# TensorE's instructions of the expert groups in one written order

## The chip, the cores and the metric

The kernel runs on one core of one Trainium2 chip. The time is the device time of one execution in microseconds (us). The core's engines, as the profile names them: TensorE (PE; the loads of its stationary operands are shown apart, as PEld), VectorE (DVE), ScalarE (ACT), GpSimd (POOL) and SyncE (SP), which issues the transfers of the weights from HBM to the on-chip memory over the DMA engines. Each engine has its own queue of instructions and works through it in order; where one engine needs a result of another, it waits at a semaphore.

## The reference, cut to what matters

Two layers (DEPTH = 2) work on x of 256 tokens x 1024 channels, all in fp32. In each, a mixer of three branches (a state-space scan, a gated spatial MLP, attention to 256 memory tokens) is added to x, then a mixture of experts, each followed by a LayerNorm. The change lies in the mixture of experts:

```python
D_MODEL, SEQ, N_GROUPS_MOE, EXP_PER_GROUP, D_EXPERT, TOP_K_INNER = 1024, 256, 4, 8, 256, 2

g_star = argmax(x @ w_rg + b_rg)                 # one of 4 groups for each token
top_v, top_i = top_k(le_sel, 2)                  # two of its 8 experts
weights = softmax over the group's choice and the two experts, zero for all others
h = silu(einsum('nd,edf->nef', x, w_gate_e)) * einsum('nd,edf->nef', x, w_up_e)
moe = einsum('nef,efd->nd', h * weights[:, :, None], w_down_e)
x = layer_norm(alpha * x + moe)
```

There are 32 experts. Each has 1024 x 256 weights for the gate, as many for the up product and 256 x 1024 for the down product: 3 MB, so 100 MB a layer, and every one is read in both layers.

## The kernel before, in words

A layer (the variable l) first computes the mixers, which fill the first half of its time, and then the experts. The **expert stage** takes the experts in 8 groups of four (the loop over g, NG = 8). Each expert has 32 slots for tokens, so that a group's 128 slots fill the 128 partitions.

**Weights.** A group's weights are 12 pieces of 128 x 2048 numbers, 1 MB each: 8 pieces for gate and up (w_gu, k = 0 to 7) and 4 for down (w_dn, two for each half hf of the 1024 output channels). `Stream` (L98 to 170) keeps the list of all pieces in order, and SP issues the DMA of a piece as soon as the ring of buffers that it belongs to has one free; `RINGS` (L188) deals the pieces out to 23 such places, in rotation. `st.done` gives a buffer free, and the next piece's DMA is issued at that place of the program.

**One group.** In the order in which the code is written:

- `pick` (L1208): VectorE writes a matrix of zeros and ones, M.S, that says which token stands in which slot (L1214, L1216).
- `gather` (L1227): TensorE multiplies it by x, 16 matmuls in the program for two halves of the channels (32 in the trace, since each fp32 matmul runs as two passes); ScalarE (L1237) and VectorE (L1239) each copy one half out of its bank of PSUM (in groups 0 and 1 they share each half, column block by column block).
- `columns` (L1258): the products with one piece, 4 matmuls of 32 x 512 in the program and 8 in the trace, one for each expert. Eight pieces add up in one bank (`hb`). After the fourth, `place_back` (L1218) turns M.S around and scatters the weights of the tokens to their slots (TensorE, with copies at L1224 and L1225).
- `hidden` (L1262): ScalarE's Silu (L1263) and VectorE's product (L1264).
- `turn` (L1266): TensorE transposes the 128 x 256 hidden values, two instructions, and ScalarE copies them out (L1269).
- Down products with pieces 0 and 1 into a bank `yb`, then `parts_of` (L1277): ScalarE copies the high part of the result (y[0], L1279), VectorE subtracts it and has the low part (y[1], L1280). The same for pieces 2 and 3.
- `combine` (L1283): TensorE multiplies the high and the low part of one half by M.ST and adds to two of the four accumulators, `accs`, 4 matmuls of 128 x 512. The half hf = 0 is combined after the down products of hf = 1, the half hf = 1 at the end of the group.

**More than 32 tokens.** Where an expert has more, an extra round runs inside `tc.If(nrv[g] > 0)`, with the same weights and a bank of its own, `xbank`. There are two such places for gate and up (L1397, after the fourth and the eighth piece) and two for down (L1435, after each half). Where no expert of the group has more than 32 tokens, every engine skips them by a branch; st.done stands behind each of them. A last place, L1447, holds third and further rounds for all groups, a long stretch of code that is skipped here; it stands at the end of group g = NG - 2.

**Banks.** Four of the eight banks are the accumulators, one is xbank, and three (`ps_bank`) serve in rotation for all else: hidden values, placing back, gather, turn, down products.

**The order.** Instructions are recorded as the code is written, but a scheduler of the language then orders each engine's queue by its own model of durations. For TensorE this is switched off by `manual_schedule` from the start of the expert stage to the end of group 0's gate and up products:

```python
order.enter_context(tc.manual_schedule(engines={mybir.EngineType.PE}))
...
for g in range(NG):
    ...
    if g == 0:
        order.close()
    if g + 1 < NG:
        xs = list(gather_group(g + 1))[0]
    turn(M, ps_bank())
```

From there on, in groups 0 (its second half) to 7, the scheduler sets TensorE's order. The other engines' queues are always ordered by it.

## Time and profile before

| | before |
|---|---|
| three runs, us | 1028.56, 1024.04, 1027.78; median 1027.78 |
| the profiled execution | time 1021.68, span 1019.5 |
| TensorE clock granted, mean of the span | 0.971 |
| busy PE | 907.1 (89%) |
| busy DVE | 577.1 (57%) |
| busy ACT | 483.1 (47%) |
| busy POOL | 28.4 (3%) |
| read from HBM | 286.24 MB, 284 GB/s on average |

The time is 2.2 us longer than the span, which goes from the first to the last instruction that the profile shows. The expert stage of layer 0 lies at about 291 to 491 us, that of layer 1 at 781 to 1007 us. In the rows further below, a line such as L215 is that of a helper (`mm`) that records every matmul; the group is known by the tiles: `ps` is a bank in rotation, `acc` an accumulator, `e_90` and `ringB` are buffers of weights, `xs` the gathered x, `late` the small tiles of the group (M.S, M.ST, hidden values), `y` the high and low parts. "x8" behind a shape counts instructions that run one after the other, the time ahead of it is from the first one's start to the last one's end, and "[idle <-ACT y L1279]" says that the engine stood idle that long before it and which instruction ended the wait. ACTq and PEq are the engines' sequencers, where branches are.

### The profile page before, as it was taken

The numbers are of one execution on the slowest core, as the hardware profiler recorded it, in microseconds if no ns is written. First come the engines' busy times: TensorE is split into PE (matmuls) and PEld (weight loads), VectorE is DVE, ScalarE is ACT, GpSimd is POOL, SyncE is SP. The second block draws the span as 40 slices with busy tenths as digits, with TensorE's granted clock in tenths as the row PEclk, the third lists the DMA queues.
The fourth block names the chain that finished last, engine by engine and source line by source line (L and its number), as shares of the span: only waits on it lengthen the run. The fifth ranks groups of instructions, "written<-read, shape, count | busy, mean of one in ns | idle before, by whom it ended". The sixth has DMA issues, their size and how long they took to land. (4 is left out here: it accounts for less than half of the span.)

```text
span 1019.5 us, 19509 instructions
## 1 busy us (share of the span) xinstructions
PE 907.1 (89%) x7726; PEld 657.2 (64%) x7726; DVE 577.1 (57%) x1233; ACT 483.1 (47%) x991; POOL 28.4 (3%) x60
## 2 busy tenths in 40 slices
PE   6999999989989998876997999999898989999863
PEld 6898998989854533321797898998885444433421
DVE  7979798776642211210898999889474221111105
ACT  6876967756433111110779697774653211111112
POOL 3001000000000000010000000000000000000001
PEclk9999999999999999987998999999999999999988
DMA  8574263459779999999792335453975999999961
GB/s 299 212 284 145 89 233 145 169 192 420 289 258 413 415 418 418 414 419 406 295 367 83 129 105 212 172 202 117 406 301 207 395 419 416 367 388 391 413 274 42
DMA packets 48084, 289.06 MB, mean 284 GB/s; under 512 B 5328, under 2 KB 6608, under 8 KB 16080
## 3 DMA queue, kind: packets, MB, share of 16 engines
q1 hardware_dynamic: 47808, 286.26, 71.7%
q8 instruction: 82, 1.34, 0.5%
q10 hardware_dynamic: 144, 1.05, 0.3%
q14 instruction: 50, 0.41, 0.1%
HBM read 286.24 MB, written 1.05 MB: 282 GB/s over the span
## 5 line engine op out<-in xcount | busy, mean ns | idle before, releaser
L336 DVE TENSOR_TENSOR wl<-ringA,wh 128x512 fp32r<-128x512 f32 x280 | 189.4, 689 | 60.7 <-ACT wh L335 57.2
L335 ACT ACTIVATE wh<-ringA 128x512 fp32r<-128x512 f32 x280 | 170.7, 629 | 89.9 <-PE acc L215 74.0
L215 PE MATMUL acc<-xh,wh 128*128 128x256 f32 x576 | 168.7, 296 | 11.7 <-ACT wh L335 11.7
L215 PE MATMUL acc<-xh,wl 128*128 128x256 f32 x576 | 168.5, 293 | 6.2 <-DVE wl L336 5.9
L215 PE MATMUL acc<-xl,wh 128*128 128x256 f32 x576 | 166.9, 290 | 0.0
L215 PEld LDWEIGHTS acc<-xh,wh 128*128 128x128 f32 x576 | 113.2, 198 | 14.7 <-ACT wh L335 12.8
L215 PEld LDWEIGHTS acc<-xh,wl 128*128 128x128 f32 x576 | 114.4, 199 | 8.5 <-DVE wl L336 7.1
L215 PEld LDWEIGHTS acc<-xl,wh 128*128 128x128 f32 x576 | 114.0, 198 | 0.5 <-issue 0.4
L215 PEld LDWEIGHTS ps<-late,xt 128*128 128x128 f32 x544 | 65.2, 198 | 23.0 <-issue 21.9
L215 PE MATMUL ps<-late,xt 128*128 128x128 f32 x544 | 69.1, 285 | 9.2 <-DVE late L1354 5.6
L215 PE MATMUL acc<-yh,wh 128*128 128x256 f32 x224 | 64.8, 292 | 7.3 <-ACT yh L1038 5.4
L1280 DVE TENSOR_TENSOR y<-ps,y 128x512 fp32r<-128x512 f32 x32 | 22.1, 692 | 84.6 <-ACTq L1435 48.1
L215 PE MATMUL acc<-yh,wl 128*128 128x256 f32 x224 | 63.9, 286 | 1.1 <-DVE wl L336 1.1
L215 PE MATMUL acc<-yl,wh 128*128 128x256 f32 x224 | 63.4, 285 | 0.0
L215 PE MATMUL acc<-y,late 128*128 128x512 f32 x144 | 48.2, 435 | 15.9 <-ACT y L1279 8.2
L215 PEld LDWEIGHTS acc<-y,late 128*128 128x128 f32 x144 | 22.8, 188 | 56.4 <-ACT y L1279 19.9
L1279 ACT ACTIVATE y<-ps 128x512 fp32r<-128x512 f32 x32 | 19.1, 598 | 83.6 <-PE ps L215 79.2
L1264 DVE SCALAR_TENSOR_TENSOR late<-ps,late 128x256 f32<-128x256 f32 x16 | 7.7, 483 | 88.0 <-ACT late L1263 88.0
L215 PEld LDWEIGHTS acc<-yh,wh 128*128 128x128 f32 x224 | 42.7, 192 | 9.8 <-ACT yh L1038 5.8
L1263 ACT ACTIVATE late<-ps 128x256 f32<-128x256 f32 x16 | 6.2, 385 | 87.3 <-PE ps L215 87.3
L215 PE MATMUL ps<-ringA,xs 128*32 128x512 f32 x248 | 38.2, 657 | 9.8 <-PEq L1447 5.8
L215 PEld LDWEIGHTS acc<-yh,wl 128*128 128x128 f32 x224 | 43.0, 192 | 2.0 <-DVE wl L336 1.9
(404 smaller groups left out, 1722.5 us busy)
## 6 DMA issues: line engine op xcount, KB each, us to landing
e<-w_gu SPq DMA_DIRECT2D x35, 1024.0 KB, 8.9
ringB<-w_gu SPq DMA_DIRECT2D x32, 1024.0 KB, 14.4
ringB<-w_dn SPq DMA_DIRECT2D x31, 1024.0 KB, 13.6
ringA<-w_gu SPq DMA_DIRECT2D x31, 1024.0 KB, 16.3
ringA<-w_gate SPq DMA_DIRECT2D x24, 1024.0 KB, 4.8
e<-w_dn SPq DMA_DIRECT2D x23, 1024.0 KB, 12.6
ringA<-w_in SPq DMA_DIRECT2D x15, 1024.0 KB, 4.9
ringA<-w_br SPq DMA_DIRECT2D x12, 1024.0 KB, 4.8
```

The source lines that it names most:

```text
L215: PE.matmul(o, lhsT, rhs, start=start, stop=stop, skip_group_check=True)
L335: A.activation(wh, w, AF.Copy)
L336: V.tensor_sub(wl, w, wh)
L1263: A.activation(r.sg, hb[:, 0:256], AF.Silu)
L1264: V.scalar_tensor_tensor(r.h, hb[:, 256:512], r.wv[:, 0:1], r.sg, op0=OP.mult, op1=OP.mult)
L1279: A.activation(yh, yb, AF.Copy)
L1280: V.tensor_sub(yl, yb, yh)
```

## The change

TensorE's order is now written by hand through all eight groups of both layers, and the code of a group is put in the order in which TensorE is to run it:

- `order.close()` moves from group 0 to behind the last combination of group 7 (to behind the loop over g).
- `turn` of a group stands between the two halves of the next group's gather (it stood behind the whole gather in the code).
- The second combination, `combine(M.ST, y, 1)`, moves from the group's end to behind the second piece (k = 1) of the next group; for group 7 it stands behind the loop.
- The third and further rounds (L1447) become a function, `last_rounds`, that is called behind that combination in group 7; they stood at the end of group 6.
- `combine` goes through the high part for both token halves and then through the low part, where it had taken high and low for one half of the tokens and then for the other.

In the changed kernel L1397 is L1409, L1435 is L1449, L1447 is L1315; the lines up to L1283 keep their numbers.

```diff
--- before.py
+++ after.py
@@ -1281,9 +1281,9 @@
                 return yh, yl
 
             def combine(ST, y, hf):
-                for t in range(2):
-                    mm(accs[t][hf], ST[:, 128 * t:128 * t + 128], y[0], False, False)
-                    mm(accs[t][hf], ST[:, 128 * t:128 * t + 128], y[1], False, False)
+                for yp in y:
+                    for t in range(2):
+                        mm(accs[t][hf], ST[:, 128 * t:128 * t + 128], yp, False, False)
 
             def more_rounds(g, y, wf):
 
@@ -1308,6 +1308,13 @@
                         for f in range(2):
                             columns(X.bank, X.hT[:, f, :], fetch(dram["w_dn"][l, g * 4 + 2 * hf + f]), f == 0, f == 1)
                         combine(X.ST, parts_of(X.bank, y), hf)
+
+            def last_rounds():
+                x_rows()
+                y = parts_tiles("wl", "wl")
+                with tc.If(nrv[NG] > 1):
+                    for i in range(NG):
+                        more_rounds(i, y, l0)
 
             accs = [[acc_bank() for _ in range(2)] for _ in range(2)]
 
@@ -1384,6 +1391,11 @@
                     W = {k: lambda e, key=("gu", l, g, k): st.chunk(key, e) for k in ks}
                     for k in ks:
                         columns(hb, xs[k // 4][:, k % 4], W[k], k == 0, k == 7)
+                        if k == 1 and g > 0:
+
+                            combine(M.ST, y, 1)
+                            if g == NG - 1:
+                                last_rounds()
                     if 2 in ks:
                         if g == 0:
                             weights()
@@ -1414,11 +1426,13 @@
                     if 2 in ks and g == PLAIN - 1:
                         Task(affine_rows(l, par, 0, dgs), 1.0)
                     step(2)
-                if g == 0:
-                    order.close()
                 if g + 1 < NG:
-                    xs = list(gather_group(g + 1))[0]
+                    nxt = gather_group(g + 1)
+                    xs = next(nxt)
+                    next(nxt)
                 turn(M, ps_bank())
+                if g + 1 < NG:
+                    next(nxt)
                 y4 = [parts_tiles("wh", "wl") for _ in range(2)]
                 for hf in range(2):
                     W = [lambda e, key=("dn", l, g, 2 * hf + f): st.chunk(key, e) for f in range(2)]
@@ -1440,13 +1454,8 @@
                         combine(X.ST, parts_of(X.bank, y4[1 - hf]), hf)
                     for f in range(2):
                         st.done(("dn", l, g, 2 * hf + f))
-                combine(M.ST, y, 1)
-                if g == NG - 2:
-                    x_rows()
-                    y = parts_tiles("wl", "wl")
-                    with tc.If(nrv[NG] > 1):
-                        for i in range(NG):
-                            more_rounds(i, y, l0)
+            combine(M.ST, y, 1)
+            order.close()
             if l + 1 < L:
                 residual(1)
             else:
```

On TensorE in layer 1, from group 6's gather to group 6's first piece, the order before was as follows (both passes of a matmul are one instruction here; `e_94` and `e_95` are group 5's down pieces of hf = 0, `e_90` and `e_91` those of hf = 1, `e_92` the first piece of group 6; what is left out is the skipped code of the extra round):

```order
L215 MATMUL ps<-late,xt 128x128 x16
L1268 MATMUL ps<-ident,late 128x128 x2
L215 MATMUL ps<-e_94,late 32x512 x4
L215 MATMUL ps<-e_95,late 32x512 x4
L1435 COMPARE_AND_BRANCH
...
L215 MATMUL acc<-y_12198,late 128x512 x2
L215 MATMUL acc<-y_12199,late 128x512 x2
L215 MATMUL ps<-e_90,late 32x512 x4
...
L215 MATMUL ps<-e_91,late 32x512 x4
L215 MATMUL acc<-y_12200,late 128x512 x2
L215 MATMUL acc<-y_12201,late 128x512 x2
L215 MATMUL ps<-e_92,xs 32x512 x4
```

The first combination stood straight behind the first skip, one down piece of hf = 1 behind the second skip, and the second combination behind that, ahead of group 6. In the changed kernel TensorE has at the same place (`e_93` is the second piece of group 6):

```order
L215 MATMUL ps<-late,xt 128x128 x8
L1268 MATMUL ps<-ident,late 128x128 x2
L215 MATMUL ps<-late,xt 128x128 x8
L215 MATMUL ps<-e_94,late 32x512 x4
...
L215 MATMUL ps<-e_90,late 32x512 x4
L215 MATMUL ps<-e_91,late 32x512 x4
L215 MATMUL acc<-y_12197,late 128x512 x2
L215 MATMUL acc<-y_12198,late 128x512 x2
...
L215 MATMUL ps<-e_92,xs 32x512 x4
L215 MATMUL ps<-e_93,xs 32x512 x4
L215 MATMUL acc<-y_12199,late 128x512 x2
L215 MATMUL acc<-y_12200,late 128x512 x2
```

The turn has moved between the halves of the gather, the first combination behind both down pieces of hf = 1, and the second behind two pieces of group 6.

VectorE's queue in layer 1, from the norm's steps (L470) to group 2's pick (L1214, L1216), before:

```order
L470 TENSOR_TENSOR xt<-xt,ringB 128x512 x6
L1264 SCALAR_TENSOR_TENSOR late<-ps,late 128x256
L1214 TENSOR_TENSOR late<-ri,late 128x512
L1216 TENSOR_TENSOR late<-late 128x256
L1239 COPY xs<-ps 128x512
```

and now:

```order
L1409 UNCONDITIONAL_BRANCH x2
L1264 SCALAR_TENSOR_TENSOR late<-ps,late 128x256
L470 TENSOR_TENSOR xt<-xt,ringB 128x512
L1214 TENSOR_TENSOR late<-ri,late 128x512
L1216 TENSOR_TENSOR late<-late 128x256
L1239 COPY xs<-ps 128x512
```

One of the eight norm steps has moved from ahead of the hidden values' product (L1264) to behind it; all eight are still ahead of the pick.

On TensorE in layer 1, the jump over the third and further rounds before:

```order
L215 MATMUL acc<-y_12412,late 128x512 x2
L215 MATMUL acc<-y_12413,late 128x512 x2
L1447 COMPARE_AND_BRANCH
L1291 COMPARE_AND_BRANCH
L1291 UNCONDITIONAL_BRANCH x2
```

and now:

```order
L215 MATMUL ps<-ringA,xs 32x512 x8
L215 MATMUL acc<-y_12411,late 128x512 x2
L215 MATMUL acc<-y_12412,late 128x512 x2
L1315 COMPARE_AND_BRANCH
L1291 COMPARE_AND_BRANCH
```

The jump stood behind the last combination of group 6, ahead of all products of group 7; now two pieces of group 7 are ahead of it.

## Rows read from the trace of the kernel before

**Rows 1.** TensorE's waits, 776 to 1020 us: for whom, us in total, times, longest.
```profile
PE acc L215 <- ACT y L1279: 5.2, 7, 0.8
...
PE ps L215 <- ACT late L1269: 3.8, 8, 0.5
PE acc L215 <- ACTq L1435: 2.9, 4, 0.7
...
PE ps L215 <- DVE late L1216: 2.4, 1, 2.4
```

**Rows 2.** Timeline of TensorE, group 5 of layer 1: start, length, out<-in, [idle <-releaser].
```profile
948.85 0.38 PE L1268 MATMUL ps<-ident,late 128*128 128x128 f32 x2
949.71 1.93 PE L215 MATMUL ps<-e,late 128*32 128x512 f32 x16 [0.47 <-ACT late L1269]
952.35 1.46 PE L215 MATMUL acc<-y,late 128*128 128x512 f32 x4 [0.72 <-ACTq L1435]
953.74 1.07 PE L215 MATMUL ps<-e,late 128*32 128x512 f32 x8
954.99 1.07 PE L215 MATMUL ps<-e,late 128*32 128x512 f32 x8 [0.18 <-PEq L1435]
956.81 1.46 PE L215 MATMUL acc<-y,late 128*128 128x512 f32 x4 [0.76 <-ACT y L1279]
958.20 1.06 PE L215 MATMUL ps<-e,xs 128*32 128x512 f32 x8
```

**Rows 3.** Stretches: busy us of PE, PEld, DVE, ACT, POOL, clock, DMA share, GB/s.
```profile
440.00:450.00 10.00, 8.29 (x56) 4.17 (x57) 0.48 (x1) 0.98 (x2) 2.18 (x3) 0.78 1.02 422
...
880.00:890.00 10.00, 9.12 (x91) 4.27 (x93) 0.69 (x1) 0.85 (x3) 0.00 (x0) 1.00 0.77 285
```

**Rows 4.** Timeline of TensorE, groups 6 and 7 of layer 0.
```profile
440.43 1.94 PE L215 MATMUL ps<-ringB,xs 128*32 128x512 f32 x8 [0.50 <-DMA ringB<-w_gu]
...
446.39 3.84 PE L215 MATMUL ps<-late,xt 128*128 128x128 f32 x32
...
487.69 1.06 PE L215 MATMUL ps<-e,late 128*32 128x512 f32 x8 [0.18 <-PEq L1435]
```

**Rows 5.** The tensor w_dn at 460 to 480 us: its last issues, time to landing.
```profile
L157 SPq DMA_DIRECT2D e<-w_dn x4: 327/328/328, 466.2 to 474.4; - x4
...
DMA to landing us min/median/max: 12.6/12.9/13.2
```

**Rows 6.** The tensor w_dn at 955 to 1000 us: its last issues, time to landing.
```profile
L157 SPq DMA_DIRECT2D e<-w_dn x4: 327/327/328, 966.7 to 970.6; - x4
...
DMA to landing us min/median/max: 12.6/13.5/16.2
```

**Rows 7.** Timeline of TensorE, the last weights' products of layer 1.
```profile
1003.89 1.06 PE L215 MATMUL ps<-e,late 128*32 128x512 f32 x8 [0.18 <-PEq L1435]
```

**Rows 8.** Timeline of TensorE, groups 2 and 3 of layer 1: steps without a wait.
```profile
867.74 1.18 PE L215 MATMUL acc<-y,late 128*128 128x512 f32 x4
868.86 1.92 PE L215 MATMUL xbank<-ringB,late 128*32 128x512 f32 x16
...
874.71 1.04 PE L215 MATMUL ps<-ringG,xs 128*32 128x512 f32 x8
875.57 1.90 PE L215 MATMUL ps<-ringA,xs 128*32 128x512 f32 x16
```

**Rows 9.** Timeline of TensorE, layer 1: turn of group 0, placing back of group 1.
```profile
799.96 0.38 PE L1268 MATMUL ps<-ident,late 128*128 128x128 f32 x2
...
812.55 0.33 PE L1221 MATMUL ps<-ident,late 128*128 128x128 f32 x1
```

**Rows 10.** Timeline of TensorE behind the jump of line 1447, layer 0 and layer 1.
```profile
464.94 0.45 PE L1221 MATMUL ps<-ident,late 128*128 128x128 f32 x1 [3.97 <-PEq L1447]
...
470.78 5.92 PE L215 MATMUL ps<-ringA,xs 128*32 128x512 f32 x26 [3.45 <-issue]
...
986.42 1.94 PE L215 MATMUL ps<-ringA,xs 128*32 128x512 f32 x8 [5.79 <-PEq L1447]
```

## The prediction, made before the changed kernel ran

> **What bounds the kernel now.** I read the list of waits of TensorE first, then its instructions in order of time, then the DMA stretches and the landing of the last weights of each layer.
>
> The list of waits covers the expert stage of layer 1. Three of its rows are one pattern: TensorE waits for ScalarE's copy of the turned hidden values (ACT late, 8 times, 3.8 us) and for the first half of a split product (ACT y, ACTq, 11 times, 8.1 us) [rows 1]. The timeline shows the pattern for one group: the turn at 948.85, down products 0.47 us later than they could start, a combination after a wait of 0.72, the second half of the down products, a combination after 0.76, and only at 958.20 the next group's products [rows 2]. At each of these places a short chain over two engines lies bare, because nothing else was queued between.
>
> Whether a faster TensorE ends the layer earlier depends on the weights. In **layer 0** it does not: the DMA share is 1.02 with 422 GB/s at 440 to 450 us [rows 3], TensorE waits there for pieces of 1 MB [rows 4], the last piece is issued at 474.4 and lands 12.6 us or a little more later, at 487.0 [rows 5], and its products start at 487.69 [rows 4]. So 0.7 us is the most that layer 0 can give. In **layer 1** the last piece is issued at 970.6 and lands at the latest 16.2 us later, at 986.8 [rows 6], but its products start only at 1003.89 [rows 7]: TensorE is 17.1 us behind its weights. The stream even pauses: 285 GB/s at 880 to 890 us [rows 3], since its buffers are full. There TensorE's own order is the bound, and time taken out of it reaches the end.
>
> **The change, part by part.** The sum is made for layer 1, on the profiled execution (span 1019.5, time 1021.68 us). That run lies 6.1 us under the median of the runs shown, 1027.78; I take the difference in us off the median.
>
> Prices without a wait: one piece's products, 8 matmuls in the trace, take 0.86 us from start to start (874.71 to 875.57); a combination takes 1.12 (867.74 to 868.86) [rows 8]; the turn 0.38 (the first of rows 2). Between two pieces with a skipped branch there are 1.25 us (953.74 to 954.99) [rows 2], so a skip costs 0.39.
>
> From the turn to the next group's products there are 32 matmuls of down products (4 x 0.86 = 3.44), two combinations (2.24), the turn (0.38) and two skips (0.78): 6.84 us. In group 5 the trace has 9.35 (948.85 to 958.20) [rows 2], so 2.5 us are waits.
>
> - *The turn between the two halves of the gather.* The copy of the turned values is done while the second half (about 1.9 us of the 3.84 that 32 gather matmuls take [rows 4]) runs. If that cover were missing, 0.47 us would come back.
> - *The first combination after both halves of the down products,* and *the second one after two pieces of the next group.* Each gets 1.7 us of other products and a skip ahead of it; the longest wait is 0.76 plus what the low half takes, 1.46 - 1.12 = 0.34 [rows 2]. If the next group's first pieces haven't landed, the combination stands behind them: in layer 1 they have.
> - *The skips.* One of the two lies inside a wait today and will be bare. That is in the sum (0.78 for two).
> - *Groups 4, 5, 6* are priced like 5: 7.5 us. *Groups 0 and 1*: the scheduler had already put part of the next group's products between. From the turn of group 0 to the placing back of group 1 there are 12.59 us (799.96 to 812.55) [rows 9] with four pieces more (3.44): 12.59 - 3.44 - 6.84 = 2.3. Group 1 I take as the same: 4.6 us for both. *Groups 2 and 3* enter the extra round (products into xbank [rows 8]), and that hid the combinations already; the turn's 0.86 - 0.38 = 0.48 is left, 1.0 us for both. *Group 7* has no gather and its last combination has nothing behind it; only the first one's wait goes: (0.92 before it, reckoned from 949.71 + 2 x 0.86, plus 0.27 in it, less the bare skip) 0.8. *Sum: 13.9 us.*
> - *The wait of 2.4 us for VectorE's pick* (DVE late L1216) [rows 1] stays: in the new order of VectorE the same eight norm steps stand ahead of that pick.
> - *The split of the combination's loop* (both high parts, then both low ones): in the later groups the scheduler had that order already. Nothing.
> - *The jump over the extra rounds* (L1447) moves behind two pieces of group 7. It leaves TensorE idle for 5.79 us in layer 1 and 3.97 in layer 0 [rows 10]. No row shows it at the new place. What is queued ahead of it there waits for nothing, as in layer 0; behind it all of group 7 waits. The bounds: 1.8 us less than now, or 3.5 more, since in layer 0 a second hole of 3.45 came soon after the jump [rows 10] and the DMA will be full there in layer 1 now too. I take half of the gain, 0.9.
> - *Layer 0*: the same savings, eaten by waits for weights; 16 small products of the norm rows are no longer strewn among others and will wait for ScalarE one by one, but in group 1, long before the first wait for weights. I take 0, between 0.7 less and 1.8 more (one piece and one combination at the low clock instead of the high one: 1.94 for 8 matmuls at 440.43 [rows 4] against 1.07, and as much again).
> - *SP's queue*: the order of loads against skips shifts by one place here and there, and in early layer 1 one w_in load passes one expert load. At one piece of 1 MB each (2.5 us) and with 0.3 to 1.0 of the DMA idle there I take nothing.
>
> Sum: 13.9 + 0.9 = 14.8 us, so the profile would have about 1004.7 and the time 1027.78 - 14.8 = **1013 us**. The stream allows it: 17.1 us of lead, more if it stops pausing.
>
> **The rivals.**
> *(a) The weights bind layer 1 too.* A buffer is free only after its last product and the skip of its half; if the stream came later by that, or waited behind a skip, the lead of 17.1 would be used up early. If the last landing slipped from 986.8 to 996, the gain would be 17.1 - 9 = 8: 1020. For it: the stream pauses only because TensorE is slow; against it: faster products free buffers earlier, and the pause is a reserve of some 3 us (10 x (1 - 285/422)) [rows 3].
> *(b) The waits only move.* Three banks serve hidden values, turn, gather and down products in rotation, and a written order cannot step round a bank that is still being emptied. The emptying copies are of the kind that now cost 0.72 to 0.76 [rows 2]. Two of these for each of seven groups would be 10.3 us back: gain 4.5, 1023. Against it: by the order of the built program each bank is reused two or three steps after its copy.
> *(c) Slower: the low clock in layer 0.* A quicker TensorE waits longer for weights, and after such waits the clock was at its lower level (0.78 on average at 440 to 450 [rows 3], 8 matmuls in 1.94 us [rows 4]). A group has 12 x 0.86 + 3.84 + 2.24 + some 2 (turn, placing back, skips) = 18.4 us of work at 2.4 GHz and about 36.8 at 1.2; its 12 pieces, 12.6 MB, take 29.8 us at 422 GB/s. If the clock stayed low from group 4 to 7, TensorE would lose 7 us on the weights in each: +28 - 14.8 = +13, so 1041. It decides from three groups on. Against it: the gather at 446.39 already ran at the high level again (32 matmuls in 3.84) [rows 4]: more work at the low clock fills the waits that lowered it. The Trainium skill, "TensorE: Matmul & The Clock Gate", section "HAM oscillation — how this bites in real kernels", says that a kernel whose matmuls wait for DMA between pieces pays the low clock at every piece. That speaks against this change, and by it the time would be that of (c); the trace has the fall, but for one stretch only, and both the products at the low clock and the weights' interval of 2.5 us leave it room.
> *(d) More than forecast.* The jump is hidden further, groups 4 and 6 had longer waits than 5, and 17.1 us or a little more come out: 1009, at best 1004.
>
> **How the numbers follow.** About 0.5%, 5 us, is what a measurement of this kernel can tell from no change. Forecast (1007 to 1018): 0.70. (a): 0.10. (d) under 1007: 0.08. (b): 0.07. (c): 0.05. Faster by over 0.5%: 0.70 + 0.10 + 0.08 = 0.88; same 0.07; slower 0.05. The range: the sum's ends are 13.9 + 1.8 + 0.7 + the rest of the 17.1 on one side, some 21 us with a run's scatter, and 13.9 - 3.5 - 1.8 = 8.6 on the other: 1005 to 1020.
>
> **What would show it.** Right: in layer 1 the waits for ACT y and ACT late fall to the extra rounds and group 7, 9.35 becomes about 6.9, the last products start near 989. In layer 0 the waits for DMA grow and the last products still start at 487. Wrong: new waits of TensorE for copies (b), a low clock beyond 480 us (c), waits for DMA in layer 1 before group 7 (a), or a jump longer than 6 us.

## The result, and the profile after

The changed kernel takes 1013.08 us (median of 4 runs, 1011.72 to 1013.59), the kernel before 1025.91 beside it (4 runs): a ratio of 0.9873, 95% interval 0.984 to 0.9905. In a second comparison it was 1010.94 against 1026.40 (0.9869, interval 0.9842 to 0.9895). The forecast was 1013. The sum behind it was right about layer 1 as a whole, wrong in some of its terms there, and it left out two losses, as the traces show.

The page of the changed kernel (span; busy time of each engine and its share):

```profile
span 1011.7 us, 19517 instructions
...
PE 893.8 (88%) x7726; PEld 664.7 (66%) x7726; DVE 577.0 (57%) x1233; ACT 480.3 (47%) x991; POOL 28.3 (3%) x60
```

TensorE's waits, 776 to 1020 us, as in [rows 1] (for whom, us in total, times, longest):

```profile
PE ps L215 <- DMA e<-w_gu: 3.5, 1, 3.5
PE ps L215 <- PEq L1409: 3.3, 7, 1.5
PE ps L215 <- DVE late L1216: 3.2, 1, 3.2
PE ps L215 <- PEq L1449: 2.8, 9, 0.4
...
PE acc L215 <- ACT y L1279: 2.2, 3, 0.7
...
PE acc L215 <- ACTq L1409: 0.7, 1, 0.7
PE ps L215 <- ACT late L1269: 0.5, 1, 0.5
```

The waits for ScalarE's turned copy have gone from 3.8 us (8 times) to 0.5 (once, group 7), those for the high half of a split product from 8.1 us (11 times) to 2.9 (2.2 + 0.7, 4 times: only in the extra rounds of groups 2 and 3). What stands now are skips that lie bare (PEq L1409, L1449), VectorE's pick for group 2, and one wait of 3.5 us put down to a weight piece, e<-w_gu: that is the jump over the third and further rounds. The product behind it reads the third piece of group 7, which SP issued at 949.6 and which landed 17.4 us later, at 967.0; the wait lasts to 978.13. In a variant with the same order there (turn_behind, below) the row names the jump itself (3.65 us, PEq L1315), and without the code of those rounds it is gone.

The same place as [rows 2], group 5 of layer 1, now reads:

```profile
944.82 0.38 PE L1268 MATMUL ps<-ident,late 128*128 128x128 f32 x2
945.04 1.95 PE L215 MATMUL ps<-late,xt 128*128 128x128 f32 x16
946.92 1.92 PE L215 MATMUL ps<-e,late 128*32 128x512 f32 x16
949.17 1.92 PE L215 MATMUL ps<-e,late 128*32 128x512 f32 x16 [0.33 <-PEq L1449]
951.03 1.19 PE L215 MATMUL acc<-y,late 128*128 128x512 f32 x4
952.52 1.92 PE L215 MATMUL ps<-e,xs 128*32 128x512 f32 x16 [0.30 <-PEq L1449]
954.38 1.20 PE L215 MATMUL acc<-y,late 128*128 128x512 f32 x4
955.50 1.07 PE L215 MATMUL ps<-ringC,xs 128*32 128x512 f32 x8
```

From the turn to the next group's products 9.35 us have become 952.52 - 944.82 = 7.70; the second half of the gather (1.88) now lies inside and the second combination (1.12) outside, so like for like it is 6.94, against 6.84 reckoned without any wait.

The end of layer 1, after:

```profile
973.40 1.20 PE L215 MATMUL acc<-y,late 128*128 128x512 f32 x4
978.13 1.93 PE L215 MATMUL ps<-ringA,xs 128*32 128x512 f32 x8 [3.53 <-DMA e<-w_gu]
...
983.96 1.94 PE L215 MATMUL ps<-ringD,xs 128*32 128x512 f32 x8 [1.48 <-PEq L1409]
...
995.24 2.52 PE L215 MATMUL acc<-y,late 128*128 128x512 f32 x8
```

The wait of 3.53 us is the jump (it was 5.79, [rows 10]), but four pieces behind it run at the lower clock (1.93 to 1.97 us for 8 matmuls, where they take 1.06 otherwise; 1.2 of 2.4 GHz) and the next skip takes 1.48 us.

**The balance of the two traces** (span 1019.5 before, 1011.7 after: 7.8 us, less than the 12.8 of the medians). The stage of layer 1, from its first gather to the end of its last combination, takes 225.78 us before and 208.91 after, 16.9 less. But it starts at 788.85 instead of 781.39, 7.5 later, and the tail (from there to the end of the span) is 13.94 us instead of 12.34. So 16.9 - 7.5 - 1.6 = 7.8.

### The profile page after: what moved, and what is told of

Read it like the earlier page. It is cut to its first block, busy times and chain, and to the rows that moved or that the text cites. A ratio compares the mean times of both kernels' runs of the same rounds, so it can differ in the third digit from the quotient of the medians.

```text
span 1011.7 us, 19517 instructions
## 1 busy us (share of the span) xinstructions
PE 893.8 (88%) x7726; PEld 664.7 (66%) x7726; DVE 577.0 (57%) x1233; ACT 480.3 (47%) x991; POOL 28.3 (3%) x60
## 5 line engine op out<-in xcount | busy, mean ns | idle before, releaser
L336 DVE TENSOR_TENSOR wl<-ringA,wh 128x512 fp32r<-128x512 f32 x280 | 189.3, 689 | 61.1 <-ACT wh L335 57.8
L215 PEld LDWEIGHTS ps<-late,xt 128*128 128x128 f32 x544 | 69.0, 205 | 26.4 <-issue 25.3
L215 PE MATMUL ps<-late,xt 128*128 128x128 f32 x544 | 73.8, 292 | 12.4 <-DVE late L1361 5.6
L1280 DVE TENSOR_TENSOR y<-ps,y 128x512 fp32r<-128x512 f32 x32 | 22.1, 691 | 59.6 <-ACTq L1449 49.1
L1224 ACT ACTIVATE late<-ps 128x256 fp32r<-128x256 f32 x18 | 6.9, 383 | 103.1 <-PE ps L215 99.2
L215 PE MATMUL ps<-ringA,xs 128*32 128x512 f32 x248 | 34.3, 662 | 18.5 <-DMA ringS<-w_gu 9.9
L215 PE MATMUL acc<-y,late 128*128 128x512 f32 x144 | 44.4, 424 | 3.4 <-ACT y L1279 2.2
L1214 DVE TENSOR_TENSOR late<-ri,late 128x512 bf16<-128x512 f32 x18 | 12.4, 688 | 55.5 <-PE ps L215 55.2
```

The source lines that it names most:

```text
L215: PE.matmul(o, lhsT, rhs, start=start, stop=stop, skip_group_check=True)
L336: V.tensor_sub(wl, w, wh)
L1214: V.tensor_tensor(r.S2, iota.unsqueeze(1).unsqueeze(1).to_broadcast([128, 2, 2, 128]), slg[:, :, :, g].unsqueeze(3).to_broadcast([128, 2, ...
L1224: A.activation(r.ST, b[:, 0:256], AF.Copy)
L1280: V.tensor_sub(yl, yb, yh)
```

## The experiments

Below, "the stage" is that of layer 1, and a group's interval goes from the start of its first down product to the next group's, from the timeline of TensorE; the last goes to the end of the last combination. Times are in us:

| kernel | to group 0 | 0 | 1 | 2 | 3 | 4 | 5 | 6 | 7 | stage | tail |
|---|---|---|---|---|---|---|---|---|---|---|---|
| before | 19.42 | 25.13 | 32.32 | 39.71 | 29.31 | 22.42 | 21.57 | 27.34 | 8.56 | 225.78 | 12.34 |
| changed | 19.11 | 23.37 | 30.38 | 38.64 | 27.49 | 19.08 | 19.02 | 25.34 | 6.48 | 208.91 | 13.94 |
| turn_behind | 19.45 | 23.88 | 30.76 | 39.18 | 27.93 | 19.53 | 19.42 | 25.21 | 6.47 | 211.84 | 13.88 |
| second_at_end | 19.06 | 21.55 | 30.07 | 38.31 | 27.13 | 18.76 | 18.70 | 26.03 | 6.49 | 206.11 | 13.94 |
| jump_back | 19.03 | 23.34 | 30.36 | 38.64 | 27.38 | 19.10 | 19.04 | 24.81 | 6.48 | 208.18 | 14.25 |
| order_only | 19.21 | 23.72 | 30.62 | 39.29 | 28.04 | 19.32 | 19.31 | 23.43 | 7.88 | 210.81 | 12.79 |
| no_jump | 19.04 | 23.39 | 30.37 | 38.64 | 27.37 | 19.08 | 19.04 | 16.69 | 10.85 | 204.46 | 14.61 |
| written_l0 | 19.06 | 24.88 | 31.96 | 39.16 | 27.92 | 21.64 | 20.83 | 27.95 | 8.56 | 221.98 | 12.37 |
| best1 | 19.06 | 21.56 | 30.07 | 38.30 | 27.03 | 18.76 | 18.70 | 23.74 | 8.21 | 205.42 | 12.53 |
| best3 | 19.06 | 18.81 | 30.05 | 38.30 | 27.03 | 18.77 | 18.71 | 24.84 | 9.08 | 204.65 | 12.54 |

Each row is one trace. Where nothing was changed, an interval repeats within 0.3 us from trace to trace, with two exceptions: group 0 moves by up to 1.8 with the clock, and group 6, which has the jump, by up to 1.2 (25.21 to 26.45 in the four traces with the whole order of the changed kernel, or all of it but the turn's place). The verdicts below rest on the stages; the times of most variants lie so close that their intervals overlap.

**Both kernels once more.**

> The changed kernel once more, unaltered, as the measure for the others. In the two traces so far the expert stage of layer 1 (first gather to the end of the last combination) takes 225.8 us before and 208.9 after, 17 us less, but everything ahead of that stage came 7.5 us later after than before. Theory: the 17 us are the change's, and most of the 7.5 us are scatter between executions, so the stage takes 208.9 +- 0.5 again, the time is 1011 to 1015, and the early drift differs. Rival: the 7.5 us belong to the change (layer 0), so the stage starts at 788.9 again within half a us.

> The kernel before once more, unaltered, for a second trace. In its first one the expert stage of layer 0 starts at 292.3 us, its last weights land at 487.0, and the stage of layer 1 starts at 781.4 and takes 225.8; in five traces of the changed kernel and its variants these starts lie at 294.9 to 295.8, 490.5 to 492.4 and 785.5 to 789.1. Theory: that trace was of an execution that was short in its early part (1021.7 us against a median of 1026), so this one has the stage of layer 1 at 225.8 +- 0.5 again but starting at 785 or later. Rival: the change delays the early part and layer 0 by 3 to 5 us; then this trace has 292, 487 and 781 again.

The changed kernel: stage 208.58, tail 13.91, stage started at 785.52. The kernel before: stage 225.83, started at 782.83, time 1024.39. So the stage's 17 us are the change's. Of the 7.5 us ahead of it a part is scatter, as the first expectation had it: the changed kernel's stage started 3.3 us sooner here. Against the second expectation, not all of it is: the stage of before started only 1.4 later than in its first trace (lost in its first 20 us) and not at 785 or later. The rest is taken apart under layer 0.

**The turn alone undone.**

> One part undone: the turn stands behind the whole gather of the next group again; all else as changed. Theory: its copy lies bare at 7 places, 0.47 us each, so the stage of layer 1 takes 208.9 + 3.3 = 212.2 and the time is 1016.5. Rival (the waits only move; something else of the change gave the gain): no difference, 209 and 1013.

```diff
                     xs = next(nxt)
                     next(nxt)
+                    next(nxt)
                 turn(M, ps_bank())
-                if g + 1 < NG:
-                    next(nxt)
```

Stage 211.84, 3.1 us longer than the two of the changed kernel (mean 208.75); time 1015.82 (ratio to before 0.9891, 0.9861 to 0.9921). The interval of group 4 is 0.45 longer, that of group 5 0.40. The theory's 212.2 was right: this term of the sum, 0.47 a group, holds.

**The second combination alone undone.**

> One part undone: the second combination stands at the end of its group again (ahead of the next group's pieces), all else as changed. As the prediction summed, this wait was 0.76 plus 0.34 us in each of groups 0, 1, 4, 5 and 6: then the stage takes 208.9 + 5.5 = 214.4, the time 1018.5. The rival, from the trace of the changed kernel: the first combination (1.2 us) and a skip (0.3) now stand behind the last down products and cover the copies (0.76 to the high part, some 1.7 to the low one) by themselves, so that it makes no difference: 209 to 210, and 1013 to 1014.

```diff
                         if k == 1 and g > 0:
-                            combine(M.ST, y, 1)
                             if g == NG - 1:
                                 last_rounds()
...
                         st.done(("dn", l, g, 2 * hf + f))
-            combine(M.ST, y, 1)
+                combine(M.ST, y, 1)
```

Neither: the stage is 206.11, 2.6 us *shorter*, the time 1008.75 (0.9833, 0.9815 to 0.9851). Group 5 to group 6 in the timeline of this kernel:

```profile
947.85 2.51 PE L215 MATMUL acc<-y,late 128*128 128x512 f32 x8
950.29 1.92 PE L215 MATMUL ps<-e,xs 128*32 128x512 f32 x16
952.03 1.04 PE L215 MATMUL ps<-ringC,xs 128*32 128x512 f32 x8
```

The two combinations run back to back without a wait. The first one (1.13) and the skip cover the copies of the second. And this order is cheaper: from the first combination to the third piece of group 6 it takes 952.03 - 947.85 = 4.18 us, the changed kernel 955.50 - 951.03 = 4.47 for the same work. There the skip costs 952.52 - 951.03 - 1.13 = 0.36 ahead of weight products, here 950.29 - 947.85 - 2.26 = 0.18 between two combinations; the other 0.12 us is the switch from products to combination and back. That is 0.3 for each of groups 1 to 5; group 6 with the jump is 0.7 longer. Of the 1.8 in group 0's interval 0.2 is of this kind; for the rest the gather at 825 us ran at the high clock here and at the low one in the changed kernel. That part is not the order's: written_l1 (below), which has the changed order in layer 1, takes 21.71 for group 0, and best1_again, with the second combination at its group's end, 23.18. So of the 2.6 us some 1.1 are the order's.

**The jump alone undone.**

> One part undone: the jump over the third and further rounds stands at the end of group 6 again, and with it that group's second combination; all else as changed. In layer 1 the jump left TensorE idle for 5.79 us there before and 3.53 after. Theory: the stage takes 208.9 + 2.3 = 211.2, time 1015. Rival: what lies queued ahead of the jump doesn't matter and the rest of it is eaten by the weights, no difference, 209 and 1013. The other way: the jump comes sooner after the skips of the extra round and is dearer, over 7 us.

```diff
-                            combine(M.ST, y, 1)
-                            if g == NG - 1:
-                                last_rounds()
+                            if g < NG - 1:
+                                combine(M.ST, y, 1)
...
+                if g == NG - 2:
+                    combine(M.ST, y, 1)
+                    last_rounds()
```

No loss: stage 208.18 (0.6 shorter than the mean of the changed kernel's two), time 1011.23 (0.985, 0.9826 to 0.9874). The timeline:

```profile
970.05 2.51 PE L215 MATMUL acc<-y,late 128*128 128x512 f32 x8
978.04 5.35 PE L215 MATMUL ps<-ringA,xs 128*32 128x512 f32 x24 [5.49 <-PEq L1315]
983.13 1.46 PE L215 MATMUL ps<-ringD,xs 128*32 128x512 f32 x8
...
985.19 1.06 PE L215 MATMUL ps<-ringD,xs 128*32 128x512 f32 x8
```

The hole is 5.49 us, 2.0 more than in the changed kernel, but less runs at the lower clock behind it (products are back at 1.06 us from 985.19 on), and the next skip leaves no wait in the rows, where it took 1.48. What the new place gains in the hole it gives back behind it. Over all traces with a written order in layer 1 the interval of group 6 is 25.2 to 26.5 us with the jump at the new place and 23.4 to 24.8 at the old one, so the new place costs something, if anything.

**The written order alone.**

> The kernel before with one part of the change alone: TensorE runs in the order of the code through all groups (the written order ends behind group 7), and nothing in the code is moved: the turn behind the whole gather, the second combination and the jump at the end of their groups. The first combination then stands behind both down products of hf = 1, where the scheduler had put it ahead of them. Theory (from the two experiments before: moving the second combination is worth nothing, the turn's place 3.1 us): the stage of layer 1 takes about 206.1 + 3.1 - 1.2 (jump at the end of group 6) = 208 us, the time is 1010 to 1013, as the whole change. Rival (the recorded sum: turn and second combination carry more than half of it): 215 us or more, 1019 or more.

```diff
-                if g == 0:
-                    order.close()
                 if g + 1 < NG:
                     xs = list(gather_group(g + 1))[0]
...
+            order.close()
             if l + 1 < L:
                 residual(1)
```

Stage 210.81, time 1013.83 (0.9881, 0.985 to 0.9911): 15.0 of the 17.0 us of the stage's gain are there with nothing moved in the code. The theory had 208, the rival 215 or more. The same place in this trace:

```profile
946.16 1.92 PE L215 MATMUL ps<-e,late 128*32 128x512 f32 x16 [0.47 <-ACT late L1269]
948.41 1.92 PE L215 MATMUL ps<-e,late 128*32 128x512 f32 x16 [0.33 <-PEq L1433]
950.26 2.52 PE L215 MATMUL acc<-y,late 128*128 128x512 f32 x8
952.72 1.92 PE L215 MATMUL ps<-e,xs 128*32 128x512 f32 x16
```

Only the turn's 0.47 is left. Both waits of the combinations are gone at once, since in the order of the code the first one stands behind both down products of its second half, and thereby covers the second. The scheduler had pulled it ahead of them, straight behind the skip, where it waits ([rows 2]). In groups 0 and 1 no wait stood at the combinations; there, in the kernel before, the scheduler had cut a piece in two to put a part of it between them. Group 1 before:

```profile
831.83 1.05 PE L215 MATMUL ps<-e,xs 128*32 128x512 f32 x2
833.02 1.17 PE L215 MATMUL acc<-y,late 128*128 128x512 f32 x4
834.12 3.63 PE L215 MATMUL ps<-e,xs 128*32 128x512 f32 x30
```

The 2 matmuls take 1.19 us up to the combination, and the other 30 of these four pieces 3.57 (to the next instruction at 837.69). In order_only all 32 stand together and take 3.57 too (835.55 to 839.12). So cutting the piece cost about as much as a wait and the slower combination behind it do elsewhere (0.76 + 0.34).

In the end there is a new wait of 1.14 us for the low half (DVE y L1280) in group 7, because VectorE's residual now comes between.

**Without the jump.**

> The changed kernel without the code of third and further rounds, which no expert needs with these inputs: no jump in either layer. Theory: in layer 1 it costs its hole (3.5 us), products at the lower clock for some 9 us after it and a dearer skip (1.4): about 8 us of TensorE; but the last weights are used only 4.1 us after they land, so the stage takes 204.6 (208.7 - 4.1) with waits for weights in group 7, and the time is 1008. Layer 0 ends with its weights as before, although a hole of 9.6 us goes there. Rival: only the hole counts, 205.2, and no waits for weights; or, if the stream comes sooner too, down to 200 and 1004.

The interval of group 6 falls from 25.3 to 16.69, by 8.6 us: 3.5 of hole and 5.1 of low clock and skip behind it. But only 4.3 reach the stage (204.46, as the theory had it; time 1005.42, 2.6 under it; ratio 0.9786, 0.9751 to 0.9821), for now the weights end last:

```profile
981.18 1.93 PE L215 MATMUL ps<-e,late 128*32 128x512 f32 x8 [0.18 <-DMA e<-w_dn]
983.91 1.93 PE L215 MATMUL ps<-e,late 128*32 128x512 f32 x8 [0.79 <-DMA e<-w_dn]
986.39 1.86 PE L215 MATMUL ps<-e,late 128*32 128x512 f32 x8 [0.55 <-DMA e<-w_dn]
```

Each of the last three pieces waits for its DMA, and the products are at the lower clock again.

**The order written in one layer only.**

> The changed kernel with the written order in layer 1 alone; in layer 0 the scheduler orders TensorE from group 0's end on, as before. In the traces so far the written order shortens the stage of layer 1 by 17 us, but from the start of layer 0's stage to the start of layer 1's the changed kernel and its variants take 0.9 to 6.4 us longer than the kernel before. Theory (the gain is layer 1's, and layer 0 gives some of it back, by first combinations that stand behind the last weights and by a lower clock around waits for weights): the stage of layer 1 takes 208.7 +- 0.5 and starts at 781 to 784, the time is 1007 to 1009, under the whole change. Rival (layer 0 gives nothing back, the later starts are scatter): 1011 to 1013 as the whole change, with the stage starting at 785 or later.

> The other half: the written order in layer 0 alone, layer 1 as the scheduler orders it. Theory: layer 0 ends with its weights all the same, so nothing is gained and 1 to 6 us are lost behind it: 1026 to 1031, with the stage of layer 1 at about 225 us. Rival: layer 0 carries a part of the gain: 1020 or less. With no loss in layer 0: 1024 to 1027.

```diff
+                if g == 0 and l == 0:
+                    order.close()
                 if g + 1 < NG:
                     nxt = gather_group(g + 1)
```

(with l == 1 for the second). Layer 1 only: 1007.31 us (0.9814, 0.9791 to 0.9836), stage 208.24, started at 783.27; all of the gain, and 3.6 and 5.8 us under the two medians of the whole change (its interval lies wholly under the two of the whole change, 0.984 to 0.9905 and 0.9842 to 0.9895). Layer 0 only: 1024.70 (0.9977, 0.996 to 0.9994), stage started at 789.63. Its stage was not the 225 expected but 221.98, so the time that would have meant no loss (1024 to 1027) doesn't mean it here: 3.8 us of stage came out as 2.6 of time. The scheduler ordered layer 1 again, but from the code with the turn between the gather's halves. Its timeline shows the turn's wait gone and the two of the combinations as they were:

```profile
954.26 1.92 PE L215 MATMUL ps<-e,late 128*32 128x512 f32 x16
956.90 1.46 PE L215 MATMUL acc<-y,late 128*128 128x512 f32 x4 [0.72 <-ACTq L1451]
958.29 1.06 PE L215 MATMUL ps<-e,late 128*32 128x512 f32 x8
...
961.36 1.46 PE L215 MATMUL acc<-y,late 128*128 128x512 f32 x4 [0.76 <-ACT y L1279]
```

So most of the 3.8 us (225.8 - 222.0) is the turn's and the combinations have the rest of the gain. How much the code's other moves have in the 3.8 is open: groups 4 and 5 gain 0.8 and 0.7, more than 0.47.

**What the order in layer 0 gives back.** From the start of layer 0's stage to the start of layer 1's there are 489.1 us in both traces of before, 489.5 in written_l1 and 489.0 in best3 (which leaves layer 0 to the scheduler). In the ten traces with the written order in layer 0 there are 489.8 to 494.2, median 492.7: 3.6 us lost, though no single trace tells how much of it is scatter.

TensorE, faster by the removed waits, catches up with the weights in layer 0 some 28 us earlier than before (its first wait for a piece ends at 407.65 in the timeline, at 435.45 before); it stands idle between pieces, and the granted clock is lower. 405 to 425 us (busy us of PE, PEld, DVE, ACT, POOL; clock, DMA share, GB/s), in the kernel before and the changed one:

```profile
405.00:425.00 20.00, 17.72 (x142) 7.47 (x140) 3.11 (x7) 2.80 (x6) 0.00 (x0) 1.00 1.02 413
```

```profile
405.00:425.00 20.00, 13.40 (x76) 4.61 (x75) 1.82 (x5) 0.77 (x2) 0.00 (x0) 0.83 1.02 415
```

The DMA share is 1.02 in both. All ten traces with the written order in layer 0 have 0.83 or less in this stretch, the four without it 1.00. But this stretch is not where the time goes: from the start of the stage to the products of the last piece the ten take 194.8 to 197.9 us (median 196.2), before 195.4 and 195.6. The weights set that end either way. In the changed kernel's trace the last piece lands at 492.43, the products start with it, and both combinations, VectorE's residual and sums now follow behind it: the first product of the next layer that needs VectorE waits 1.75 us there (DVE wl L336) and 0.80 before. Then the first products of the next layer run at the lower clock. 500 to 505 us, before and changed:

```profile
500.00:505.00 5.00, 5.00 (x42) 4.90 (x41) 3.22 (x6) 3.37 (x6) 0.00 (x0) 1.00 0.91 365
```

```profile
500.00:505.00 5.00, 5.00 (x33) 5.00 (x33) 4.50 (x8) 1.28 (x3) 0.00 (x0) 0.72 0.85 283
```

The loss goes with the clock here. Over 490 to 510 us it is 1.00 in the four traces without the written order in layer 0 and in the two of the ten that lost least (489.8 and 490.1), 0.95 and 0.92 in the next two (490.2 and 491.2), and 0.83 to 0.91 in the other six (492.5 to 494.2). No run changed this stretch by itself, so that the clock there is the cause is likely and not shown. The jump's hole in layer 0 is not the cause: no_jump, which has none, is among the six (492.9).

**A version from the parts that paid.** best1: written order, turn between the gather's halves, second combination and jump at the group's end as before, and in group 7 the first combination between the two down products. best3: as best1, but layer 0 left to the scheduler, and group 2's pick moved ahead of the norm's steps. The diff has what best3 adds to order_only and turn, the last piece of it being best1's.

> A version made of what the experiments favour: written order through all groups, the turn between the halves of the gather, second combination and jump at the end of their groups as before, and in group 7 the first combination between the two down products of hf = 1, so that VectorE has its residual and sums (2.5 us) done before the last combination; in the changed kernel these stand behind it and the tail from the last combination to the end is 13.9 us against 12.3 before. Theory: stage 206.1 - 1.2 + 1.0 = 205.9 us, tail 12.3, time 1007 to 1009, 3 to 5 under the changed kernel. Rival: the places don't add up, stage 208 and tail 13.9, time 1011 to 1013.

> best1 once more, beside best3: stage 205.4 +- 0.6, tail 12.5, time 1005 to 1008. If the stage's length hung on one stretch of low clock at 825 us, which best1 and the version with the second combination at its group's end did not have, it may come out at 207.

> The version best1 with two more steps: layer 0 is left to the scheduler, and group 2's pick is written right behind group 1's placing back, ahead of the norm's steps, so that group 2's gather waits only for these (it waited 3.2 us; the pick is 1.1 of the chain). Theory: the stage of layer 1 starts at 781 to 784 and takes 205.4 less at most 1.0, since in best1 the last weights were used only 0.9 us after they landed: 204.4 to 205.4; time 1001 to 1004. Rival (layer 0's order costs nothing): 1005 to 1006, as best1.

```diff
             def gather_group(g, n=4):
-                pick(g, slg0, M)
+                if g != PLAIN:
+                    pick(g, slg0, M)
...
                         place_back(M, ps_bank())
+                        if g + 1 == PLAIN:
+                            pick(PLAIN, slg0, M)
...
+                if g == 0 and l == 0:
+                    order.close()
...
                     for f in range(2):
                         columns(yb, M.hT[:, f, :], W[f], f == 0, f == 1)
+                        if hf == 1 and f == (g < NG - 1):
+                            combine(M.ST, y, 0)
```

best1 takes 1005.94 us (0.9803, 0.9773 to 0.9832) and 1008.75 in the second comparison (0.9817, 0.9782 to 0.9851), with stages of 205.42 and 207.31: as the expectation said, the 2 us lie in the stretch at 825 us, 21.56 against 23.18 for group 0's interval. best3 takes 1004.10 (0.9779, 0.9748 to 0.9811), 4.6 under best1 in the same comparison, though the two intervals overlap; its stage started at 783.98. The pick's move took the whole wait of 3.2 us and the low clock behind it (group 0's interval 18.81), more than the 1.1 expected, but the stage is only 204.65, since its last pieces wait for weights:

```profile
982.53 1.06 PE L215 MATMUL ps<-e,late 128*32 128x512 f32 x8 [1.06 <-DMA e<-w_dn]
...
985.02 1.06 PE L215 MATMUL ps<-e,late 128*32 128x512 f32 x8 [0.30 <-DMA e<-w_dn]
```

The last piece is used 0.05 us after it lands (984.97).

## Why the prediction was right, and where it was not

**TensorE's order as layer 1's bound: right.** The lead of 17.1 us over the weights fell to 4.1 (990.15 landed, 994.25 used). The stream came sooner too: the last landing is 201.3 us after the stage's start instead of 205.4, so the pause of [rows 3] was a reserve, as rival (a)'s counter-argument had it. The last products start 205.4 us after the stage's start instead of 222.5.

**The sum for layer 1: 14.8 forecast, 16.9 and 17.2 measured.** By intervals (forecast, then before less changed): group 0 2.3 and 1.8; 1 2.3 and 1.9; 2 0.5 and 1.1; 3 0.5 and 1.8; 4 2.5 and 3.3; 5 2.5 and 2.6; 6 with the jump 3.4 and 2.0; 7 0.8 and 2.1. Group 4 was mis-sized by pricing it like 5. There the scheduler had also put a skip into the middle of a piece:

```profile
942.97 1.06 PE L215 MATMUL ps<-ringS,xs 128*32 128x512 f32 x6
944.23 1.02 PE L215 MATMUL ps<-ringS,xs 128*32 128x512 f32 x2 [0.19 <-PEq L1397]
945.18 3.84 PE L215 MATMUL ps<-late,xt 128*128 128x128 f32 x32
```

From the piece to the gather this took 2.21 us; in the changed kernel, where the skip stands behind the whole piece, it takes 1.45 (941.51 to 942.96). That is the 0.8. For groups 0 and 1 the prediction had 2.3 each by subtraction, without a cause; a cut piece was 1.2 of it. In 7 both waits of the combinations went and not one; 3 was not taken apart.

**The turn: right,** 0.47 a group forecast, 3.3 for seven; 3.1 us measured by undoing it, and at most 3.8 by written_l0.

**The second combination: the step failed as a cause.** "The second one after two pieces of the next group" was credited with a wait of up to 0.76 + 0.34. Moving it does nothing for that wait; the first combination's place removes both, and the new place costs 0.3 us a group. The sum came out because the two waits had been added, whoever removed them. The prediction had the rows to see it: a chain of 0.76 us behind 1.12 us of combination and a skip.

**The jump: the step failed.** Of the 0.9 us credited nothing was measured (0.6 the other way). The prediction priced the hole and not the clock behind it, which [rows 10] showed: 8 products in 1.94 us after the hole. In layer 0 the hole grew to 9.64 us from 7.4 (3.97 + 3.45, [rows 10]), beyond the 6 us that the prediction had named as a sign of being wrong; there the weights end last all the same (the last piece lands at 492.43 and is used at 492.47). The Trainium skill, "Runtime: NRT & Kernel Launch", section "Instruction fetch mechanics", says that a taken branch whose target lies outside the loaded window has to fetch its instructions by DMA before execution goes on. That fits: the skips inside a group cost 0.2 to 0.4 us, this one over a much longer piece of code 3.5 to 10.9. The traces don't separate fetching from other costs of a branch.

**Layer 0: mis-sized.** Forecast 0, with 1.8 us as the worst; the ten traces have a median of 3.6 lost and up to 5. The products of the last piece did not start at 487 but at 492.47, 1.9 later counted from the stage's start (197.3 us instead of 195.4). The step that failed is that savings "eaten by waits for weights" end with these: most of the loss came behind the last weights, where the prediction had no term. Its own sign for rival (c), a low clock beyond 480 us, is there (0.91 over 490 to 510 us), but for a stretch, not from group 4 to 7 throughout.

The Trainium skill, "TensorE: Matmul & The Clock Gate", section "HAM oscillation — how this bites in real kernels", which the prediction cites, has the direction: matmuls that wait for DMA between pieces meet the low clock. In the changed kernel's trace not every piece did (8 matmuls took 1.07 us at 407.65 and 1.93 at 410.79), and the change lost some 3.6 us in layer 0, not the 28 of rival (c).

**The end of the kernel: overlooked.** The tail behind the last combination grew by 1.6 us (12.34 to 13.94; 13.91 in the second trace). VectorE after (start, length), around the last combination, which ends at 997.77:

```profile
996.05 0.69 DVE L1280 TENSOR_TENSOR y<-ps,y 128x512 fp32r<-128x512 f32 x1 [1.46 <-ACTq L1449]
996.90 1.29 DVE L1368 SCALAR_TENSOR_TENSOR xt<-xt,acc 128x512 f32<-128x512 f32 x2 [0.15 <-DVEq L1449]
998.10 1.28 DVE L1372 BATCH_NORM_STATS2 bns<-xt 128x6 f32<-128x512 f32 x2
999.29 1.27 DVE L1368 SCALAR_TENSOR_TENSOR xt<-xt,acc 128x512 f32<-128x512 f32 x2
```

And before, where it ended at 1007.18:

```profile
1002.52 1.29 DVE L1361 SCALAR_TENSOR_TENSOR xt<-xt,acc 128x512 f32<-128x512 f32 x2 [0.59 <-PE acc L215]
1003.72 1.28 DVE L1365 BATCH_NORM_STATS2 bns<-xt 128x6 f32<-128x512 f32 x2
1005.70 0.69 DVE L1280 TENSOR_TENSOR y<-ps,y 128x512 fp32r<-128x512 f32 x1 [0.70 <-ACT y L1279]
1006.98 1.29 DVE L1361 SCALAR_TENSOR_TENSOR xt<-xt,acc 128x512 f32<-128x512 f32 x2 [0.59 <-PE acc L215]
```

Before, the residual and sums of the first half (1.29 + 1.28) were done between the two combinations; now they stand between the last copy of a low part and the second half's residual. The prediction counted the first combination's wait of group 7 as a gain and did not ask who waits for that combination. best1's repair of it moved 1.4 us back and cost 1.7 in the stage (8.21 against 6.48): for group 7 both orders are worth the same.

So the forecast's 14.8 us stand for 17.0 in layer 1, less 1.6 at the end and some 3.6 in layer 0: 11.8, where the medians gave 12.8 and 15.5. Two us too little gain and five too little cost cancelled in part. That the time came out at 1013.08 is luck besides: the forecast took 14.8 us off 1027.78, but beside the changed kernel the one before took 1025.91, and the gain was 12.8. The fast end of the range, too, is looser than it looks: the terms named for it come to 17.1 us, so 1011, and the way from there to 1005 was left to a run's scatter.

What stays open: a stretch of low clock at 230 to 235 us (0.82 in the changed kernel's trace, 0.58 to 0.90 in nine of the twelve traces that are not of the kernel before, best3 too) and in neither of before, ahead of everything that the change moves on TensorE. It was not tried apart.

## What to carry to other kernels

Before crediting a move with a wait, ask which other move covers the same chain: undoing parts one by one showed that of three moves one was worth 3.1 us, one nothing, and one cost time. A scheduler that puts an instruction as early as its operands' model allows can expose a chain that plain code order hides, or cut a piece in two. When the bound moves in one stage only, write the order in that stage only: the layer bound by its weights lost by it. And price a hole on TensorE with the products at the lower clock behind it, also where the hole comes after the last weights.

## What the runs showed of the hardware that was not expected

- A branch over a long stretch of skipped code idled TensorE for 3.5 to 5.9 us in layer 1 and for 9.6 to 10.9 in one hole in layer 0 (in four traces of the written order; without the jump TensorE waits for weights there). In layer 1 the whole of it was worth 8.6 us with the slower products and the dearer skip behind it; moving it by two pieces changed its parts and did not make it cheaper.
- A part of a piece costs as much as the whole: 2 of the 8 matmuls that stood alone took 1.2 us, and the other 30 of the four pieces 3.57, like all 32 together.
- A skip cost 0.36 us ahead of weight products and 0.18 between two combinations (group 5).
- With waits of 0.3 to 2.1 us between pieces of 1 MB, the granted clock over 405 to 425 us was 0.83 or less in all ten traces that had them there, and 1.00 in the four that had not.
